# A hybrid decoder block on one core: the chunked delta rule multiplies its state by the keys themselves, and its last inverse level works in 64x64 blocks

## The chip, the core and the metric

The kernel runs on one core of a Trainium2 chip. The metric is the device time of one execution in microseconds. A difference of under 0.5%, about 8.6 us here, is about what a measurement of this kernel can't tell from no change.

## What is computed

One layer of a decoder block on 1024 positions of 1024 channels: an input projection, a gated delta rule (4 heads, 128 channels each), a sparse attention, a gated merge, a LayerNorm, a convolutional feed-forward part and a second LayerNorm. Only the delta rule is touched. Cut to it, the reference reads:

```python
gc = jnp.cumsum(g, axis=-1)                     # decay, summed within a chunk
diff = gc[..., :, None] - gc[..., None, :]
decay = jnp.where(tril, jnp.exp(jnp.where(tril, diff, 0.0)), 0.0)
kk = jnp.einsum('bhnid,bhnjd->bhnij', k, k)
a_mat = jnp.where(strict, kk * decay * beta[..., :, None], 0.0)
lhs = jnp.eye(c) + a_mat
rhs = jnp.concatenate([v * beta[..., None], k * (beta * jnp.exp(gc))[..., None]], -1)
sol = lax.linalg.triangular_solve(lhs, rhs, left_side=True, lower=True)
u0, kcd = sol[..., :dv], sol[..., dv:]
...
def step(state, xc):                            # over the chunks, in order
    u = u0_c - kcd_c @ state
    o = qd_c @ state + qk_c @ u
    state = state * gl_c + kd_c.T @ u
    return state, o
```

The kernel works in chunks of 128 positions, which gives the same result.

## The kernel before

TensorE's order is written by hand (`tc.manual_schedule(engines=MS)`, with TensorE alone in `MS`); the other engines' orders come from the scheduler of the framework, and each engine works strictly in its order.

The delta rule is cut into eight units: four heads `h` by two halves `hf` of four chunks. A unit has a preparation (`pre`, a generator) and a scan (`scan`, another), each of which stops at every `yield`. Between their pieces TensorE works on the input projection: a tile of it (a "fill", `proj_gen`) is 48 products of 512 columns in three passes of a split into a high and a low part (`xTh,wh`, `xTl,wh`, `xTh,wl`). `PLAN` says which fills belong to which of nine stretches (two to four fills each), and the tables `PRE` and `SCAN` say at which fraction of a stretch a piece of the preparation or the scan is put between the fills' products: unit n's preparation begins with stretch n, its scan in stretch n+1. A fill of q, k or v channels (`act_gen`) ends with a convolution on VectorE.

A preparation transposes k (L488), spreads the gates along rows with four products by the triangle `triu` (L504), builds the strictly lower triangular matrix `Am` (L523), inverts its 16x16 diagonal blocks on VectorE (L534 to L550, over two DMA round trips), and then builds the inverse `Z` of the whole 128x128 matrix in three levels of 16, 32 and 64 (L586 to L607). Each level is two groups of four products, one for each chunk:

```python
mm(ps[:, csl[c]], Am[:, c, :], Z[:, c, :])      # then times the level's mask, on VectorE: Y
mm(ps[:, csl[c]], X[:, c, :], Y[:, c, :])       # X = Z transposed; then Z = Z + this, on VectorE
```

Behind the last level the preparation multiplies the gated keys `kb` by the inverse (L610), and ScalarE copies the result, `kc`, out. The scan then takes for each chunk, with two stops, `u = Z v + kc S` as two products into one place (L625, L627), a copy of `u` on ScalarE (L629), the product `kd u` and the new state `S` from it on VectorE (L633, L638), and the two products of the output (L640, L642).

A name pair such as `sm<-Z,Am` in a row of TensorE is the output, the moving operand and the stationary operand (which the weight load brings in). One fp32 product is two records of a matmul in the trace.

## Time and profile before

| what | us |
|---|---|
| three runs | 1714.35, 1717.88, 1722.87 (median 1717.88) |
| the profiled execution, its time | 1719.78 |
| its span from the first to the last instruction | 1718.0 |
| TensorE busy in the span | 1675.0 (97%) |

The span leaves 1.8 us of the profiled execution's time around it. A busy TensorE is not TensorE at its peak: the ends of matmuls are modelled, and neighbours overlap, so what one more product costs is read from the starts of the instructions around it and not from its own duration.

### The profile page before, as it was taken

How to read it: one execution, taken by the hardware profiler on the slowest of the kernel's cores; microseconds unless marked ns; L12 is line 12 of the kernel's file. 1: busy time of each engine (PE TensorE's matmuls, PEld its weight loads, DVE VectorE, ACT ScalarE, POOL GpSimd, SP SyncE). 2: the span in 40 equal slices, each digit the busy share in tenths (PEclk: the TensorE clock that was granted, in tenths of full speed). 3: DMA queues.
4: the chain of work that ended last, by engine and by line, in shares of the span. 5: the costliest groups of instructions: out<-in, count | busy, mean ns of one | idle time of the engine just before them, and what ended most of it. 6: DMA issues, size and time to landing. Idle time of an engine off the chain costs nothing.

```text
span 1718.0 us, 23466 instructions
## 1 busy us (share of the span) xinstructions
PE 1675.0 (97%) x8562; PEld 1411.7 (82%) x8562; DVE 1116.2 (65%) x2089; ACT 734.2 (43%) x1269; POOL 788.1 (46%) x640
## 2 busy tenths in 40 slices
PE   8999999999999998999999999999999999999997
PEld 8888888888888877888877887788888888888885
DVE  3545647657433358899874328988677667865656
ACT  3422323223222458788843115544444444443333
POOL 1322222232212537887657236678877777210005
PEclk9999999999999999999999999999999999999998
DMA  5222121221221312334125612333332232687722
GB/s 177 75 63 76 56 66 45 61 75 33 87 81 52 98 63 96 126 105 132 35 87 184 224 58 89 111 107 116 118 104 93 98 112 98 215 315 269 234 88 98
DMA packets 199024, 189.88 MB, mean 111 GB/s; under 512 B 19656, under 2 KB 155005, under 8 KB 198909
## 3 DMA queue, kind: packets, MB, share of 16 engines
q1 hardware_dynamic: 198909, 188.39, 34.3%
q8 instruction: 67, 1.10, 0.3%
q14 instruction: 48, 0.39, 0.1%
HBM read 136.97 MB, written 51.38 MB: 110 GB/s over the span
## 4 chain that ended last, share of the span: by engine, by line
PE 82%; DVE 7%; issue 3%; ACT 3%; POOL 3%; DMA 2%; SPq 0%; ACTq 0%; POOLq 0%; DVEq 0%
PE pq L193 37%; PE big L193 29%; PE sm L193 12%; PE sm L983 2%; DVE st L917 1%; ACT P L919 1%; POOL P L872 1%; DVE wh L991 1%; DMA w<-in_w_out_dram 1%; DVE wl L991 1%; DVE st L881 0%; DVE wb L1454 0%; DMA w<-in_w_down_dram 0%; DMA wsum<-w 0%; PE big L247 0%
## 5 line engine op out<-in xcount | busy, mean ns | idle before, releaser
L183 POOL TENSOR_TENSOR wl<-w,wh 128x1024 fp32r<-128x1024 f32 (+2 forms) x51 | 123.1, 2418 | 362.1 <-PE big L193 132.9
L193 PE MATMUL big<-xTl,wh 128*128 128x512 f32 x608 | 244.1, 402 | 0.0
L193 PE MATMUL big<-xTh,wh 128*128 128x512 f32 x608 | 244.1, 401 | 0.0
L193 PE MATMUL pq<-wd 128*128 128x512 f32 x924 | 209.6, 389 | 0.0
L193 PEld LDWEIGHTS pq<-wd 128*128 128x128 f32 x924 | 173.4, 188 | 36.0
L193 PE MATMUL pq<-xb,wb 128*128 128x512 f32 x792 | 187.6, 391 | 2.0 <-DVE accs L1465 1.5
L1465 DVE SCALAR_TENSOR_TENSOR accs<-pq,fcw,accs 128x510 f32<-128x510 f32 (+3 forms) x264 | 144.5, 568 | 61.0 <-ACT accs L1553 56.1
L193 PEld LDWEIGHTS pq<-xb,wb 128*128 128x128 f32 x792 | 148.5, 188 | 34.8 <-issue 2.8
L193 PE MATMUL big<-xTh,wl 128*128 128x512 f32 x608 | 160.3, 399 | 0.0
L193 PEld LDWEIGHTS big<-xTl,wh 128*128 128x128 f32 x608 | 114.7, 189 | 20.7 <-issue 0.2
L193 PEld LDWEIGHTS big<-xTh,wh 128*128 128x128 f32 x608 | 114.7, 189 | 20.6
L193 PE MATMUL pq<-mTh,wb 128*128 128x512 f32 x528 | 127.6, 397 | 3.2 <-ACT mTh L1253 3.1
L193 PEld LDWEIGHTS big<-xTh,wl 128*128 128x128 f32 x608 | 110.9, 188 | 21.4
L193 PE MATMUL pq<-mTl,wb 128*128 128x512 f32 x528 | 127.3, 391 | 0.0
L872 POOL TENSOR_TENSOR P<-P,st 128x640 f32<-128x640 f32 (+6 forms) x94 | 106.3, 1160 | 45.1 <-DVE st L881 19.7
L193 PEld LDWEIGHTS pq<-mTh,wb 128*128 128x128 f32 x528 | 101.1, 192 | 25.8 <-ACT mTh L1253 3.3
L193 PEld LDWEIGHTS pq<-mTl,wb 128*128 128x128 f32 x528 | 99.1, 188 | 21.2
L1454 POOL TENSOR_TENSOR wb<-w,wb 128x512 fp32r<-128x512 f32 x79 | 103.7, 1319 | 27.2 <-ACT wb L1253 27.2
L182 ACT ACTIVATE wh<-w 128x1024 fp32r<-128x1024 f32 (+2 forms) x51 | 53.1, 1046 | 134.8 <-PE big L193 90.7
L193 PE MATMUL big<-kS,qS 128*128 128x320 f32 (+5 forms) x384 | 86.7, 343 | 3.2 <-ACT P L919 2.0
L919 ACT ACTIVATE P<-big,st 128x640 f32<-128x640 f32 (+6 forms) x112 | 83.3, 749 | 10.3 <-DVE st L917 9.5
L1253 ACT ACTIVATE wb<-w 128x512 fp32r<-128x512 f32 x85 | 53.3, 629 | 80.3 <-PE pq L193 76.0
(394 smaller groups left out, 3558.1 us busy)
## 6 DMA issues: line engine op xcount, KB each, us to landing
w<-in_w_in_dram SPq DMA_DIRECT2D x40, 512.0 KB, 3.9
w<-in_w_up_dram SPq DMA_DIRECT2D x36, 512.0 KB, 3.8
w<-in_w_down_dram SPq DMA_DIRECT2D x53, 256.0 KB, 3.7
wsum<-w SPq DMA_DIRECT2D x44, 256.0 KB, 2.5
sig<-th SPq DMA_DIRECT2D x32, 256.0 KB, 2.2
w<-sig SPq DMA_DIRECT2D x30, 256.0 KB, 3.3
wx<-in_w_up_dram SPq DMA_DIRECT2D x11, 512.0 KB, 3.8
gdrC<-accs SPq DMA_DIRECT2D x11, 512.0 KB, 2.6
```

The costliest lines, as they stand in the source:

```text
L182: A.activation(wh[:, :n], w[:, :n], AF.Copy)
L183: G.tensor_tensor(wl[:, :n], w[:, :n], wh[:, :n].bitcast(F32), op=OP.subtract)
L193: PE.matmul(o, a, b, start=start, stop=stop, skip_group_check=True)
L872: G.tensor_tensor(p, p, r.to_broadcast([128, p.shape[1]]), op=OP.mult)
L917: V.reduce_max(nm, pv if m > 1 else pv[:, 0], axis=AX.X, negate=True)
L919: A.activation(P[:, r0 + i, :n], pv[:, i], AF.Exp, bias=nm[:, i:i + 1], accum_out=su[:, i:i + 1])
L983: PE.transpose(tp[:n, r * 128:(r + 1) * 128], P[:, r, c0:c0 + n], ident)
L991: V.tensor_tensor(pl, tp[:n], ph.bitcast(F32), op=OP.subtract)
L1253: A.activation(o, i, AF.Copy)
L1454: e.tensor_tensor(H.tile[:, 1], src(), H.tile[:, 0].bitcast(F32), op=OP.subtract)
L1465: V.scalar_tensor_tensor(o, i, fcw[:, 2 - s, j:j + 1], o, op0=OP.mult, op1=OP.add)
```

## The change

Three edits in the delta rule, and the two tables of places.

1. **The state times the keys.** `kb` (POOL), its product with the inverse (four products), and the copy `kc` are gone. `kc` is now a copy of the transposed keys, made by ScalarE from SBUF. In the scan a chunk begins with the product of the state by `kc`, VectorE adds it, times the gate `nb`, to `vb` (a new `scalar_tensor_tensor`), and after one more stop the inverse is multiplied by that sum. So a chunk has three stops in place of two.
2. **Rows of gates.** At the start of the program the summed gates are split into a high and a low part, transposed once, and laid out as `grow` (64 rows by 512). A unit then makes its rows with one product of 512 columns by a selecting matrix `pick` of ones and zeros, in place of a copy on ScalarE (`gb`) and four products by `triu`.
3. **The last level in blocks of 64.** The masked whole products of level 64 become four transposes of 64x64, four products of 64 columns by `Am`, a copy of both, four products of 64x64 and a copy of the result into the upper right block of `Z`. The transposes of the whole `Z` after level 32, and two passes of VectorE with the mask, are gone.

`PRE` has 12 places in place of 14, `SCAN` 15 in place of 11, closer together. Some small tiles move to another pool (left out of the diff).

```diff
@@ -32,8 +32,8 @@
 Y0, Y1 = 10, 12
 WOS = [4, 5, 6, 7, 8, 9, 10, 11]
 UNITS = [(t, g) for t in (1, 2, 3, 4, 5, 6, 7, 0) for g in range(2)]
-PRE = [0.0, 0.04, 0.07, 0.1, 0.14, 0.2] + [0.72 + 0.05 * i for i in range(8)]
-SCAN = [1.13 + 0.085 * i for i in range(8)] + [1.81, 1.86, 1.92]
+PRE = [0.0, 0.04, 0.07, 0.1, 0.14, 0.2] + [0.74 + 0.06 * i for i in range(6)]
+SCAN = [1.11 + 0.058 * i for i in range(12)] + [1.82, 1.87, 1.93]
 
 
 def PLAN(z, M, QKV, F):
...
@@ -271,14 +271,14 @@
...
-    triu = gmask.tile([128, 128], F32, name="triu")
+    triu = xin.tile([128, 128], F32, name="triu")
...
-    for b in (16, 32, 64):
+    for b in (16, 32):
...
@@ -381,6 +381,22 @@
     V.tensor_tensor(egd, plv, gc, op=OP.subtract)
     A.activation(egd, egd, AF.Exp)
     A.activation(egc, gc, AF.Exp)
+    gcs = xin.tile([128, 2, NT, 4], F32R, name="gcs")
+    V.tensor_copy(gcs[:, 0], gc)
+    V.tensor_tensor(gcs[:, 1], gc, gcs[:, 0].bitcast(F32), op=OP.subtract)
+    both = xin.tile([64, 32], F32, name="both")
+    V.tensor_tensor(both, ident[:64, 0:32], ident[:64, 32:64], op=OP.add)
+    pick = gmask.tile([64, 2, 2, 4], F32R, name="pick")[:, 0]
+    pick32 = xin.tile([64, 2, 4], F32, name="pick32")
+    V.reduce_sum(pick32, both.rearrange("p (f c h) -> p f h c", f=2, c=4), axis=AX.X)
+    V.tensor_copy(pick, pick32)
+    chunk = xin.tile([64, 4], F32, name="chunk")
+    V.reduce_sum(chunk, both.rearrange("p (f c h) -> p c f h", f=2, c=4), axis=AX.XY)
+    ps = sm()
+    PE.transpose(ps[:64, :128], gcs.rearrange("p l t h -> p (l t h)").bitcast(F32), ident)
+    grow = gmask.tile([64, 4, 128], F32R, name="grow")
+    V.tensor_tensor(grow, ps[:64, None, :128].to_broadcast([64, 4, 128]),
+                    chunk[:, :, None].to_broadcast([64, 4, 128]), op=OP.mult)
 
     mhalf = const.tile([128, 1], F32, name="mhalf")
     V.memset(mhalf, -0.5)
@@ -497,11 +513,8 @@
             V.tensor_tensor(nb, bp, egc[:, cs, h], op=OP.mult)
             V.tensor_scalar(bv, bv, 0.5, None, op0=OP.mult)
             yield
-            gb = g5("tmp", 3)
-            A.activation(gb, gg[:, cs, h, None].to_broadcast([128, 4, 128]), AF.Copy)
             gr = sm()
-            for c in range(4):
-                mm(gr[:, csl[c]], gb[:, c, :], triu)
+            mm(gr, pick[:, hf, h:h + 1].to_broadcast([64, 128]), grow.rearrange("p c i -> p (c i)"))
             dS = g5("tmp", 3)
             for c in range(4):
                 V.scalar_tensor_tensor(dS[:, c], gr[:, csl[c]], gc[:, hf * 4 + c, h:h + 1], mds,
@@ -578,12 +591,12 @@
                 mm(kq[:, csl[c]], kT[:, tsl[c]], qT[:, tsl[c]])
             qk = g5("qk")
             V.tensor_tensor(qk, v4(kq), dT, op=OP.mult)
-            kb = g5("tmp", 3)
-            G.tensor_tensor(kb, kt, bc(nb), op=OP.mult)
+            kc = gp.tile([128, 512], F32, name="kc", tag="kc", bufs=2)
+            A.activation(kc, kT[:, hf * 512:(hf + 1) * 512], AF.Copy)
             kd = kt
             G.tensor_tensor(kd, kd, bc(egd[:, cs, h]), op=OP.mult)
             yield
-            for b in (16, 32, 64):
+            for b in (16, 32):
                 ps = sm()
                 for c in range(4):
                     mm(ps[:, csl[c]], Am[:, c, :], Z[:, c, :])
@@ -594,27 +607,27 @@
                 for c in range(4):
                     mm(ps[:, csl[c]], X[:, c, :], Y[:, c, :])
                 V.tensor_tensor(Z, v4(ps), Z, op=OP.add)
-                if b < 64:
+                if b == 16:
                     X = g5("X")
-                if b < 32:
                     V.transpose(X.rearrange("p c i -> p (c i)"), Z.rearrange("p c i -> p (c i)"))
                 yield
-                if b == 32:
-                    ps = sm()
-                    for c in range(4):
-                        PE.transpose(ps[:, csl[c]], Z[:, c, :], ident)
-                    A.activation(X, v4(ps), AF.Copy)
-                    yield
             ps = sm()
             for c in range(4):
-                mm(ps[:, csl[c]], kb[:, c, :], Z[:, c, :])
-            kc = g5("kc")
-            A.activation(kc, v4(ps), AF.Copy)
-            st[hf] = (Z, vb, kc, qk, qd, kd, rr, rq2)
+                PE.transpose(ps[:64, c * 64:c * 64 + 64], Z[:64, c, :64], ident[:64, :64])
+            for c in range(4):
+                mm(ps[:64, 256 + c * 64:320 + c * 64], Am[:, c, :64], Z[:, c, 64:])
+            XY = g5("X").rearrange("p c i -> p (c i)")
+            A.activation(XY[:64], ps[:64], AF.Copy)
             yield
+            ps = sm()
+            for c in range(4):
+                mm(ps[:64, c * 64:c * 64 + 64], XY[:64, c * 64:c * 64 + 64], XY[:64, 256 + c * 64:320 + c * 64])
+            A.activation(Z[:64, :, 64:], ps[:64, :256].rearrange("p (c i) -> p c i", c=4), AF.Copy)
+            st[hf] = (Z, vb, kc, nb, qk, qd, kd, rr, rq2)
+            yield
 
         def scan(h, hf, st):
-            Z, vb, kc, qk, qd, kd, rr, rq2 = st[hf]
+            Z, vb, kc, nb, qk, qd, kd, rr, rq2 = st[hf]
             S = st.get("S")
             o = sm()
             for c in range(4):
@@ -622,9 +635,12 @@
                     us = sm()
                 b0 = (c % 2) * 256
                 u_ps, s_ps = us[:, b0:b0 + 128], us[:, b0 + 128:b0 + 256]
-                mm(u_ps, Z[:, c, :], vb[:, c, :], True, S is None)
+                vn = vb[:, c, :]
                 if S is not None:
-                    mm(u_ps, kc[:, c, :], S, False, True)
+                    mm(s_ps, kc[:, csl[c]], S)
+                    V.scalar_tensor_tensor(vn, s_ps, nb[:, c:c + 1], vb[:, c, :], op0=OP.mult, op1=OP.add)
+                yield
+                mm(u_ps, Z[:, c, :], vn)
                 u = gp.tile([128, 128], F32, name="u", tag="u", bufs=2)
                 A.activation(u, u_ps, AF.Copy)
                 yield
```

What moves in TensorE's order is shown at unit 1. Before, its last level stands so between the fills' products (`big<-xTh` and `big<-xTl`; L605 transposes `Z`, L488 the keys of the next unit):

```order
L605 MATMUL sm<-ident,Z 128x128 x4
L193 MATMUL big<-xTh_83,wl 128x512 x7
L193 MATMUL big<-xTh_85,wl 128x512 x3
L193 MATMUL sm<-Z,Am 128x128 x4
L193 MATMUL big<-xTh_85,wl 128x512 x5
L488 MATMUL sm<-ident,sil 128x128 x4
L193 MATMUL big<-xTh_83,wh 128x512
L193 MATMUL big<-xTl_84,wh 128x512
L193 MATMUL big<-xTh_83,wh 128x512
L193 MATMUL sm<-Y,X 128x128 x4
```

In the changed kernel the same place reads (L616 are the transposes of 64x64, `sm<-X` the four products of 64x64, `grow,pick` the rows of gates of the next unit):

```order
L616 MATMUL sm<-ident,Z 64x64 x4
L193 MATMUL sm<-Z,Am 64x64 x4
L193 MATMUL big<-xTh_85,wl 128x512 x3
L504 MATMUL sm<-ident,sil 128x128 x4
L193 MATMUL big<-xTh_83,wh 128x512
L193 MATMUL big<-xTl_84,wh 128x512
L193 MATMUL big<-xTh_83,wh 128x512
L193 MATMUL big<-xTl_84,wh 128x512
L193 MATMUL big<-xTh_83,wh 128x512
L193 MATMUL big<-xTl_84,wh 128x512
L193 MATMUL sm<-X 64x64 x4
L193 MATMUL sm<-grow,pick 128x512
```

The two groups of the level are now short ones, the whole products by `X` have gone, and the one product by `pick` stands where four by `triu` stood. The tile of the array that the built program names is 64x64 for `ident,Z` and `sm<-X`, 128x64 (rows by columns) for the `Z,Am` between fills here, 64x128 for `grow,pick`, and 128x128 for the other rows of these two pieces.

The second place is the scan of the same unit on TensorE. Before, one chunk from the product with the state (`S,kc`) to the products that read `u`:

```order
L193 MATMUL sm<-vb,Z 128x128
L193 MATMUL sm<-S,kc 128x128
L193 MATMUL big<-xTh_85,wl 128x512 x4
L193 MATMUL big<-xTh_83,wh 128x512
L193 MATMUL big<-xTl_84,wh 128x512
L193 MATMUL big<-xTh_83,wh 128x512
L193 MATMUL big<-xTl_84,wh 128x512
L193 MATMUL big<-xTh_83,wh 128x512
L193 MATMUL big<-xTl_84,wh 128x512
L193 MATMUL big<-xTh_83,wh 128x512
L193 MATMUL big<-xTl_84,wh 128x512
L193 MATMUL sm<-u,kt 128x128
```

After, from the same product to the product with the inverse, and the fills behind it:

```order
L193 MATMUL sm<-S,kc 128x128
L193 MATMUL big<-xTh_85,wl 128x512 x7
L193 MATMUL big<-xTh_83,wh 128x512
L193 MATMUL big<-xTl_84,wh 128x512
L193 MATMUL sm<-vb,Z 128x128
L193 MATMUL big<-xTh_83,wh 128x512
L193 MATMUL big<-xTl_84,wh 128x512
L193 MATMUL big<-xTh_83,wh 128x512
L193 MATMUL big<-xTl_84,wh 128x512
```

`vb,Z` no longer stands beside `S,kc` but nine products of the fills later, since it now reads what VectorE makes of `S,kc`.

The third place is VectorE while unit 4's scan meets the convolution of a fill (`sil`). The new rows are L641; L654 is the state update that was L638, L568 the transpose of `Z` that waits for a DMA:

```order
L654 SCALAR_TENSOR_TENSOR S<-S,egl,sm 128x128
L475 SCALAR_TENSOR_TENSOR sil<-big,gcw,sil 128x509
L641 SCALAR_TENSOR_TENSOR vb<-sm,sc,vb 128x128
L479 SCALAR_TENSOR_TENSOR sil<-th,sil 128x512
L545 COPY XB<-eye 32x256
L475 SCALAR_TENSOR_TENSOR sil<-big,gcw,sil 128x512 x2
L568 STREAM_TRANSPOSE X<-Z 128x512
L475 SCALAR_TENSOR_TENSOR sil<-big,gcw,sil 128x512
L654 SCALAR_TENSOR_TENSOR S<-S,egl,sm 128x128
L479 SCALAR_TENSOR_TENSOR sil<-th,sil 128x512
L641 SCALAR_TENSOR_TENSOR vb<-sm,sc,vb 128x128
```

Each chunk now has two rows of the scan on this engine, with the convolution's rows between them.

## Rows read from the trace of the kernel before

**Rows 1.** The page: span, the line of the engines' busy times, and the first line of the chain that ended last (shares of the span by engine).

```profile
span 1718.0 us, 23466 instructions
...
PE 1675.0 (97%) x8562; PEld 1411.7 (82%) x8562; DVE 1116.2 (65%) x2089; ACT 734.2 (43%) x1269; POOL 788.1 (46%) x640
...
PE 82%; DVE 7%; issue 3%; ACT 3%; POOL 3%; DMA 2%; SPq 0%; ACTq 0%; POOLq 0%; DVEq 0%
```

**Rows 2.** Busy time of each engine in the stretch from 55 to 540 us, which holds the whole delta rule (start, end, length, then busy us and records of PE, PEld, DVE, ACT, POOL, then granted clock, DMA share and GB/s).

```profile
55.00:540.00 485.00, 483.89 (x2662) 414.46 (x2662) 265.47 (x716) 136.43 (x228) 120.19 (x72) 1.00 0.22 63
```

**Rows 3.** Who kept TensorE's matmuls (first line) and its weight loads (other lines) waiting between 50 and 560 us: us in total, times, longest.

```profile
PE sm L193 <- DVE Z L596: 1.0, 2, 0.5
...
PEld sm L193 <- DVE Z L596: 1.9, 2, 0.9
PEld sm L193 <- ACT tmp L501: 0.5, 1, 0.5
```

**Rows 4.** TensorE in order of time, at a group of four full fp32 products between products of the projection (start us, duration us, then the instruction; x8 counts records, two for each fp32 product).

```profile
135.41 0.39 PE L193 MATMUL big<-xTl,wh 128*128 128x512 f32 x1
135.63 1.05 PE L193 MATMUL sm<-Y,X 128*128 128x128 f32 x8
136.44 0.48 PE L193 MATMUL big<-xTh,wh 128*128 128x512 f32 x1
136.76 0.39 PE L193 MATMUL big<-xTl,wh 128*128 128x512 f32 x1
```

**Rows 5.** The same at a group of four 128x128 transposes.

```profile
150.90 0.40 PE L193 MATMUL big<-xTl,wh 128*128 128x512 f32 x1
...
151.82 0.39 PE L193 MATMUL big<-xTl,wh 128*128 128x512 f32 x1
152.05 0.60 PE L559 MATMUL sm<-ident,sil 128*128 128x128 f32 x4
152.40 0.48 PE L193 MATMUL big<-xTh,wh 128*128 128x512 f32 x1
152.72 0.40 PE L193 MATMUL big<-xTl,wh 128*128 128x512 f32 x1
```

**Rows 6.** The same at two fp32 products whose stationary operand has 64 columns and whose moving operand has 64 (x4: two records for each), in the attention's compression after the delta rule; the last line is their weight loads.

```profile
616.24 0.40 PE L193 MATMUL sm<-xTh,wh 128*128 128x512 f32 x1
616.57 0.45 PE L193 MATMUL sm<-w2s,hTc 128*64 128x64 f32 x4
616.94 0.50 PE L193 MATMUL sm<-xTl,wh 128*128 128x512 f32 x1
617.28 0.40 PE L193 MATMUL sm<-xTh,wh 128*128 128x512 f32 x1
...
616.57 0.31 PEld L193 LDWEIGHTS sm<-w2s,hTc 128*64 128x64 f32 x4 [0.36 <-issue]
```

**Rows 7.** The same at one transpose of 32 rows, before the delta rule.

```profile
50.47 0.40 PE L193 MATMUL big<-xTl,wh 128*128 128x512 f32 x1
50.79 0.24 PE L329 MATMUL sm<-ident,st 32*128 32x32 f32 x1
50.97 0.51 PE L193 MATMUL big<-xTh,wh 128*128 128x512 f32 x1
51.31 0.40 PE L193 MATMUL big<-xTl,wh 128*128 128x512 f32 x1
```

**Rows 8.** Three state updates of the scan, each as the product that it waits for on TensorE and its start on VectorE; for the first and the last also the next product that reads the new state (start us, duration us, the instruction).

```profile
387.45 0.38 PE L193 MATMUL sm<-u,kt 128*128 128x128 f32 x2
389.33 0.34 DVE L638 SCALAR_TENSOR_TENSOR S<-S,egl,sm 128x128 f32<-128x128 f32 x1
391.32 0.39 PE L193 MATMUL sm<-S,kc 128*128 128x128 f32 x2
...
429.63 0.39 PE L193 MATMUL sm<-u,kt 128*128 128x128 f32 x2
430.06 0.35 DVE L638 SCALAR_TENSOR_TENSOR S<-S,egl,sm 128x128 f32<-128x128 f32 x1 [0.84 <-PE sm L193]
...
436.30 0.38 PE L193 MATMUL sm<-u,kt 128*128 128x128 f32 x2
438.85 0.31 DVE L638 SCALAR_TENSOR_TENSOR S<-S,egl,sm 128x128 f32<-128x128 f32 x1
440.17 0.39 PE L193 MATMUL sm<-S,kc 128*128 128x128 f32 x2
```

**Rows 9.** Groups of instructions by line and shape (xcount | busy us, mean ns of one | idle before, releaser).

```profile
L591 DVE TENSOR_TENSOR Y<-sm,lev 128x512 f32<-128x512 f32 x24 | 16.6, 691 | 69.2 <-PE sm L193 69.2
L638 DVE SCALAR_TENSOR_TENSOR S<-S,egl,sm 128x128 f32<-128x128 f32 x24 | 8.1, 338 | 21.7 <-PE sm L193 21.7
...
L612 ACT ACTIVATE kc<-sm 128x512 f32<-128x512 f32 x8 | 4.8, 595 | 3.3 <-PE sm L193 3.3
```

**Rows 10.** The start of the delta rule's work: the first product of the second fill on TensorE and the first convolution passes of the first fill on VectorE (start us, duration us).

```profile
57.05 0.39 PE L193 MATMUL big<-xTh,wh 128*128 128x512 f32 x1
...
57.98 2.32 DVE L459 SCALAR_TENSOR_TENSOR sil<-big,gcw,sil 128x511 f32<-128x511 f32 x3 [2.01 <-ACT sil L456]
```

More of the change, by code (lines that the diff above doesn't have):

```diff
@@ L222, in hybrid_block_kernel @@
     vS = S6.tile([128, NT, 2, 4, 64], F32R, name="vS", tag="s")
-    sp = gmask.tile([128, NT, 32], F32, name="sp")
+    sp = xin.tile([128, NT, 32], F32, name="sp")
     def load_x(tt):
@@ L346, in hybrid_block_kernel @@
     dtb = row_bcast(gdn_dt_bias, 4, "dtb")
-    av = ctile("av", [NT, 4])
+    av = xin.tile([128, NT, 4], F32, name="av")
     V.tensor_tensor(av, sp[:, :, 28:32], dtb[:, None, :].to_broadcast([128, NT, 4]), op=OP.add)
-    s0 = ctile("s0", [NT, 4])
-    s1 = ctile("s1", [NT, 4])
-    s2 = ctile("s2", [NT, 4])
-    s3 = ctile("s3", [NT, 4])
+    s0 = xin.tile([128, NT, 4], F32, name="s0")
+    s1 = xin.tile([128, NT, 4], F32, name="s1")
+    s2 = xin.tile([128, NT, 4], F32, name="s2")
+    s3 = xin.tile([128, NT, 4], F32, name="s3")
     A.activation(s0, av, AF.Abs)
```

## Prediction

> **What bounds the kernel now.** I read the page first: TensorE is busy for 97% of the span, and 82% of the chain that ended last is its own [rows 1]. A share over the whole span says nothing of one stage, so I took the stretch of the delta rule alone. From 55 to 540 us TensorE is busy for 483.9 of 485.0 us, at a granted clock of 1.00, while VectorE works 265, ScalarE 136 and POOL 120 us [rows 2]. The waits agree: in that stretch TensorE waited about 1 us for VectorE, its weight loads 1.9 us, and 0.5 us once for ScalarE's copy of the gates (L501) [rows 3]. So the projection's fills hide the whole chain of preparation and scan. A product taken from TensorE here is worth its slot, and work taken from another engine is worth nothing by itself. What follows the delta rule has the same order of instructions on TensorE in both kernels, and should only move earlier.
>
> **What a slot costs.** I read the starts of neighbours, not durations. Products of the fills start every 0.23 us (150.90 to 151.82, four steps) [rows 5]. A group of four whole fp32 products lengthens the way between two fill products from two steps (0.46) to 1.35 us (135.41 to 136.76): 0.89 us [rows 4]. Four whole transposes take 0.90 - 0.46 = 0.44 us in the same way [rows 5].
>
> **What is removed, per unit.** Both groups of level 64, the product with `kb`, and the four products by `triu`: 4 x 0.89 = 3.56 us, and the transposes of `Z`, 0.44: together 4.00, for eight units 32.0 us.
>
> **What is added.** Per unit one product by `pick`, 512 columns like a fill's, 0.23 us, and short ones: four transposes (one record each) and eight fp32 products (two records each), 20 records of 64 columns. The nearest row is the group of 64-column products: its four weight loads take 0.31 us together [rows 6], so a record takes at most 0.08; half of a whole product's record (0.89 / 8 / 2) is 0.055. I take 0.06, since the group's loads include a first one that overlaps nothing. So 0.23 + 20 x 0.06 = 1.43 per unit, 11.4 us in all. The scan keeps its number of products; they only stand apart.
>
> **The price of a new shape.** That group of 64-column products costs 617.28 - 616.24 - 0.46 = 0.58 us, of which four records are 0.24. The other 0.34 lies at its two edges: the fill ahead is followed after 0.33 us and not 0.23, and the weight load waits 0.36 us as issue [rows 6]. One transpose of 32 rows shows the same from the row side: 0.84 - 0.46 = 0.38, less 0.06, is 0.32 [rows 7]. So each change of the array's tile costs about 0.17 us. In the order of the changed kernel I count 49 of them: three at every pair `ident,Z` and `Z,Am`, three at every pair of `sm<-X` and `grow,pick`, and two each for the first `pick` and the last `sm<-X`, which stand alone. That makes 8.3 us. It is the term that I trust least: the rows show groups of one shape between fills, none with a second shape inside.
> The Trainium skill (TensorEngine Tiling (Array Packing), Tiling Modes) says that changing the tiling mode, and not just the tile, drains TensorE. By it the inner changes count too, as I have counted them; were only the edges of the 17 groups paid, the term would be 17 x 0.34 = 5.8 us, and no run here tells the two apart yet.
>
> **The new round trip.** In 28 chunks the product with the state must now go through VectorE before the inverse can use it. The new pass has the shape of the state's update, 0.34 us [rows 9]; sixteen passes of 0.69 us like `Y` go away with the level, so VectorE's load stays [rows 9]. What counts is the wait of TensorE, with all fills queued behind it. With nothing ahead of it, the update starts 0.43 us after its product [rows 8], so a trip needs 0.43 + 0.34 = 0.77 us. In the piece of unit 1 shown, nine fill products stand between `S,kc` and `vb,Z`: 9 x 0.23 + 0.22 for the product itself (a quarter of 0.89) = 2.29 us. That leaves 1.5 us for other rows of VectorE. Where a convolution is queued, an update started 1.88 us after its product, and at 436.30 one started 2.55 us after: held up by 1.45 and 2.12 us [rows 8]. The second would have stalled TensorE by 0.6 us in the new spacing; it is the worst that I found against its room. Twice as many such trips, with the convolution's rows between them (the third place in the order), might meet this two to four times: I take 2 us. Bounds: none, and 28 x 0.6 = 17 us.
>
> **Costed at nothing, and what covers it.** ScalarE gives up three passes of 0.6 us per unit (L612 is one [rows 9]) and gets two and a short one; POOL loses `kb`. Both have slack [rows 2]. At the start VectorE's first convolution stands behind `grow`, which waits for a transpose 13 products into the second fill: 57.05 + 3.0, so about 3 us after its old start at 57.98 [rows 10]. Two banks and a fill of 48 x 0.23 = 11 us cover that; without that cover the price is 1 us by estimate. The wait for L501 (0.5 us) goes [rows 3].
>
> **The sum.** 32.0 - 11.4 - 8.3 = 12.3 us off TensorE; less 2 for stalls, plus 0.5, less 0.3 for the start: 10.5 us. From the profiled execution, 1719.8 us (span 1718.0 [rows 1] and 1.8 around it), that is 1709.3. The median of the three runs is 1717.9, 1.9 lower, and gives 1707.4. I say 1708.
>
> **Rivals.**
> *The short products bring nothing.* If a record of 64 columns keeps the slot of a whole one (0.11), 20 of them cost 2.2 us and the added part 19.4 in place of 11.4. Then 10.5 - 8 = 2.5 us remain: 1715, no change that can be told. For it: edges are dear. Against it: the four loads in 0.31 us [rows 6]. The same end is reached if stalls take 6 us more.
> *A change of tile is free in this place*, because neighbours overlap in the queue: 10.5 + 8.3 = 18.8 us, 1699. Against it: both groups that show a change pay for it [rows 6, 7].
> *Slower: VectorE becomes the scan's bound.* Its mechanism is the new pass queued behind convolution passes, three units of which meet a scan, and behind the transpose that waits for a DMA. The gain of 12.3 us is used up at 12.3 / 28 = 0.44 us of stall per trip, and the kernel is slower by over 0.5% (8.6 us) from 0.75 us each: about 1727. For it: two hold-ups of 1.45 and 2.12 us [rows 8]. Against it: TensorE waits for hardly anything now [rows 3], and most trips fall where VectorE is half idle [rows 2].
>
> **Chances and range.** A gain of 8.6 to 15 us, the forecast: 0.50. More, with cheap changes of shape: 0.09. Under 8.6 us either way, with dear short products or stalls: 0.35. Slower by more: 0.06. So faster 0.59, the same 0.35, slower 0.06, with 0.5% (8.6 us) as the bound that a measurement can tell. The range of 1700 to 1715 leaves out the slower case, the part of the third case without a gain, and the far end of the cheap one: some 0.2 together.
>
> **What will show it.** Right: from 55 us to the scan's end some 10 us less, later stages unchanged in length; `sm<-X` groups that cost about 0.6 to 0.8 us between fills; TensorE's waits for VectorE's L641 of 1 to 4 us in total. Wrong: waits for L641 above 8 us, which would be the slower rival; short groups at 0.9 us or more, the first rival; short groups at 0.5 us with no longer step at their edges, the second.

## The result, and the profile after

The changed kernel takes 1708.05 us (median of 7 runs, 1702.83 to 1712.13) against 1718.99 us for the kernel before on the same chip (7 runs, 1714.35 to 1726.0). The ratio is 0.9919, with a 95% interval of 0.9902 to 0.9935: 0.65 to 0.98% faster. (The two medians alone lie 10.9 us apart, 0.64%, just below the small end of that interval.) The profiled execution took 1708.62 us, its span is 1706.9 us.

The page after, in the lines that answer to [rows 1]:

```profile
span 1706.9 us, 23176 instructions
...
PE 1661.8 (97%) x8443; PEld 1391.5 (82%) x8443; DVE 1118.6 (66%) x2106; ACT 734.0 (43%) x1269; POOL 778.1 (46%) x630
```

TensorE lost 13.2 us of busy time, VectorE gained 2.4. (The line of the chain is left out: in this trace the chain can be followed back only to 531 us, near the end of the delta rule, so its shares add up to 67% of the span and can't be set beside those of before.)

In the stretch of [rows 2] TensorE is still all but full, at a granted clock of 1.00:

```profile
55.00:540.00 485.00, 482.89 (x2597) 403.72 (x2596) 271.61 (x743) 138.84 (x232) 114.94 (x66) 1.00 0.23 65
```

So the stage must have become shorter, and two marks show by how much. What I call the stage below reaches from the first fill product to the first product `sm<-wh,Ck`, which stands behind the scan. On TensorE's timeline of the kernel after:

```profile
44.87 0.50 PE L193 MATMUL big<-xTh,wh 128*128 128x512 f32 x1
...
545.06 0.28 PE L193 MATMUL sm<-wh,Ck 128*128 128x256 f32 x1
```

and of the kernel before:

```profile
45.08 0.51 PE L193 MATMUL big<-xTh,wh 128*128 128x512 f32 x1
...
557.17 0.28 PE L193 MATMUL sm<-wh,Ck 128*128 128x256 f32 x1
```

500.2 us after, 512.1 before: 11.9 us. The span is 11.1 us shorter. Behind the mark every engine has the same instructions in the same order in both kernels, and the attention took 255.4 us after and 255.6 before.

Who kept TensorE waiting between 50 and 560 us (first two lines: its products; the others: its weight loads; us in total, times, longest), against [rows 3]:

```profile
PE sm L583 <- DVE sil L479: 1.7, 1, 1.7
PE sm L677 <- DVE tmp L672: 0.3, 1, 0.3
...
PEld sm L616 <- issue: 2.9, 8, 0.4
...
PEld sm L193 <- DVE S L654: 1.3, 3, 0.5
```

VectorE's new pass (L641) is not in the list. What came in are other waits: the transposes of v (L583) once wait for the end of v's convolution (L479), three products wait for the state's update (L654), and eight times the weight loads of the 64x64 transposes (L616) begin late by `issue`, as the load at the new tile shape of [rows 6] did.

### The profile page after: what moved, and what is told of

Read it like the earlier page. It is cut to its first block, busy times and chain, and to the rows that moved or that the text cites. A ratio compares the mean times of both kernels' runs of the same rounds, so it can differ in the third digit from the quotient of the medians.

```text
span 1706.9 us, 23176 instructions
## 1 busy us (share of the span) xinstructions
PE 1661.8 (97%) x8443; PEld 1391.5 (82%) x8443; DVE 1118.6 (66%) x2106; ACT 734.0 (43%) x1269; POOL 778.1 (46%) x630
## 4 chain that ended last, share of the span: by engine, by line
PE 48%; DVE 8%; issue 3%; POOL 3%; ACT 3%; DMA 2%; SPq 0%; POOLq 0%; DVEq 0%; ACTq 0%
PE pq L193 35%; PE big L193 7%; PE sm L193 5%; PE sm L999 2%; DVE st L933 1%; ACT P L935 1%; DVE wh L1007 1%; DVE wl L1007 0%; DVE wb L1470 0%; DMA wsum<-w 0%; DMA w<-in_w_out_dram 0%; DVE st L897 0%; POOL h L1327 0%; POOL h L1328 0%; DVE accs L1481 0%
## 5 line engine op out<-in xcount | busy, mean ns | idle before, releaser
L193 PE MATMUL big<-xTh,wl 128*128 128x512 f32 x608 | 164.7, 402 | 0.0
L935 ACT ACTIVATE P<-big,st 128x640 f32<-128x640 f32 (+6 forms) x112 | 83.2, 748 | 10.8 <-DVE st L933 10.2
```

The costliest lines, as they stand in the source:

```text
L193: PE.matmul(o, a, b, start=start, stop=stop, skip_group_check=True)
L935: A.activation(P[:, r0 + i, :n], pv[:, i], AF.Exp, bias=nm[:, i:i + 1], accum_out=su[:, i:i + 1])
```

## The experiments

The stage is the finer measure: it differs by 0.3 us between two profiles of one and the same kernel (first edit alone, below; the only repeat), where the timed medians of two groups of ten runs of that kernel, on two chips, lie 4.3 us apart. It has one blemish. In four of the profiles (group taken apart; full tiles; no third edit; fewer shapes, v later) TensorE waited once for 1.92 to 2.44 us inside the stage, and its granted clock was then 0.50 (1.2 GHz) for 3.4 us. That is worth up to 1.7 us of these four stages; the others, before and changed among them, ran at 1.00 throughout. All results in one table; ratios are against the kernel before on the same chip.

| kernel | stage, us | against before | time, us | ratio, 95% interval |
|---|---|---|---|---|
| before | 512.1 | | | |
| changed | 500.2 | -11.9 | 1708.05 | 0.9919 (0.9902 to 0.9935) |
| first edit alone | 505.9 | -6.2 | 1720.99 | 1.0001 (0.9988 to 1.0015) |
| the same once more | 506.2 | -5.9 | 1716.66 | 0.9965 (0.9951 to 0.9980) |
| second edit alone | 509.3 | -2.8 | 1721.13 | 0.9998 (0.9981 to 1.0016) |
| third edit alone | 514.4 | +2.3 | 1723.84 | 1.0025 (1.0010 to 1.0039) |
| group taken apart | 522.2 | +10.1 | 1727.17 | 1.0035 (1.0015 to 1.0054) |
| fewer shapes | 498.9 | -13.2 | 1707.72 | 0.9929 (0.9906 to 0.9953) |
| full tiles | 508.4 | -3.7 | 1713.73 | 0.9962 (0.9946 to 0.9978) |
| two passes | 504.3 | -7.8 | 1714.65 | 0.9966 (0.9951 to 0.9981) |
| shifted | 505.5 | -6.6 | 1712.77 | 0.9961 (0.9947 to 0.9975) |
| no third edit | 503.2 | -8.9 | 1706.73 | 0.9917 (0.9899 to 0.9935) |
| fewer shapes, v later | 502.0 | -10.1 | 1709.10 | 0.9927 (0.9912 to 0.9942) |
| tight scan | 503.0 | -9.1 | 1710.83 | 0.9939 (0.9916 to 0.9961) |

**Each edit alone, in the kernel before.** First the state times the keys, with its places:

```
-            kb = g5("tmp", 3)
-            G.tensor_tensor(kb, kt, bc(nb), op=OP.mult)
+            kc = gp.tile([128, 512], F32, name="kc", tag="kc", bufs=2)
+            A.activation(kc, kT[:, hf * 512:(hf + 1) * 512], AF.Copy)
...
+                    mm(s_ps, kc[:, csl[c]], S)
+                    V.scalar_tensor_tensor(vn, s_ps, nb[:, c:c + 1], vb[:, c, :], op0=OP.mult, op1=OP.add)
+                yield
+                mm(u_ps, Z[:, c, :], vn)
```

> The kernel before with the first edit alone: the state times the keys, VectorE's pass, and the scan spread over fifteen places; the gates' products by `triu` and the level of 64 stay as they were. Theory (slots removed, less stalls): four whole products per unit go, 8 x 0.89 = 7.1 us, no tile shape changes, one to three us of stalls come in: the first product `sm<-wh,Ck` behind the scan, which starts at 557.2 us in the kernel before, starts at 551 to 553, and the time is 4 to 6 us shorter. Rival (VectorE becomes the scan's bound): the 28 trips cost 0.44 us each or more, so the stage is as long as before or longer, and TensorE waits 12 us or more for the pass of VectorE on the state's product.

The stage is 6.2 us shorter, and TensorE all but never waits for VectorE's pass (one weight load, 0.2 us): the slots are there, nearly in full. The time did not follow; I come back to that below.

The second, the rows of gates:

```
-            gb = g5("tmp", 3)
-            A.activation(gb, gg[:, cs, h, None].to_broadcast([128, 4, 128]), AF.Copy)
...
-                mm(gr[:, csl[c]], gb[:, c, :], triu)
+            mm(gr, pick[:, hf, h:h + 1].to_broadcast([64, 128]), grow.rearrange("p c i -> p (c i)"))
```

> The kernel before with the second edit alone: the rows of gates by one product with `pick`, everything else as before. Theory: 8 x (0.89 - 0.23) = 5.3 us of slots go, 16 changes of tile shape at 0.17 us cost 2.7, and 0.5 us of wait for the copy of the gates goes: the first `sm<-wh,Ck` at 554 us, 3 us earlier than 557.2. Rival (a change of shape is free): 5.8 us earlier, 551.4. In the time neither can be told from no change; the trace decides.

The stage is 2.8 us shorter, as the theory had it. The time did not follow here either; the attention of this profile took 259.9 us, 4.3 more than before.

The third, with twelve places and one for `kb`:

```
-            for b in (16, 32, 64):
+            for b in (16, 32):
...
+                PE.transpose(ps[:64, c * 64:c * 64 + 64], Z[:64, c, :64], ident[:64, :64])
+                mm(ps[:64, 256 + c * 64:320 + c * 64], Am[:, c, :64], Z[:, c, 64:])
```

> The kernel before with the third edit alone: the level of 64 in blocks, everything else as before. Theory: eight whole products and four whole transposes per unit go, 8 x (1.78 + 0.44) = 17.8 us; 20 short records per unit come, 9.6 us by 0.06 each; 40 changes of tile shape at 0.17 us, 6.8 us: 1.4 us earlier, the first `sm<-wh,Ck` at 555.8. Rival (changes are free): 8.2 us earlier, 549. Rival (a short record costs what a whole one does, 0.11): 6.6 us later, 563.8.

2.3 us longer, which none of the three had. TensorE's weight loads show why, in one line:

```profile
PEld sm L193 <- ACT tmp L501: 6.8, 8, 1.2
```

[Rows 3] had 0.5 us here, once; now it is all eight units (the products themselves waited 3.1 us in five of them). ScalarE copies the gates (L501) behind the square of the keys (L491), and that starts when VectorE has copied the transposed keys (L489). VectorE's copy and ScalarE around one of them:

```profile
204.12 0.69 DVE L489 COPY kt<-sm 128x512 f32<-128x512 f32 x1 [5.06 <-PE sm L488]
203.89 0.37 ACT L612 ACTIVATE Z<-sm 64x256 f32<-64x256 f32 x1
204.84 0.60 ACT L491 ACTIVATE tmp<-sm 128x512 f32<-128x512 f32 x1 [0.58 <-DVE kt L489]
205.34 0.62 ACT L501 ACTIVATE tmp<-gg 128x512 f32<-128x512 f32 x1
```

and TensorE, whose product by `triu` starts at 206.01 and not at 205.3:

```profile
205.08 0.40 PE L193 MATMUL big<-xTl,wh 128*128 128x512 f32 x1
206.01 1.16 PE L193 MATMUL sm<-triu,tmp 128*128 128x128 f32 x8 [0.54 <-ACT tmp L501]
```

The level's own copy (L612) is not what holds them up: it ends at 204.26, and ScalarE is then idle for 0.58 us. What has changed is TensorE's order. Before, four whole products of the level (`sm<-Y,X`) stood between the keys' transposes and the products by `triu`; now fill products stand there alone, six at this place, which is less time than the copies need. The places that I chose put the group and the keys' transposes next to each other, so the wait belongs to this order as much as to the edit. It goes some way to explain why the three single gains (6.2 + 2.8 - 2.3 = 6.7 us) add up to less than the whole (11.9): the second edit does away with the very copy that is late here. The seven changes of shape fewer that the whole has, against the single edits together, are another part (1.2 us at 0.17 each).

**The price of a new shape.** The same work, the group taken apart, each piece at a place of its own (`PRE` has as many more places):

```
                 PE.transpose(ps[:64, c * 64:c * 64 + 64], Z[:64, c, :64], ident[:64, :64])
+                yield
             for c in range(4):
                 mm(ps[:64, 256 + c * 64:320 + c * 64], Am[:, c, :64], Z[:, c, 64:])
+                if c < 3:
+                    yield
```

> The changed kernel with the group `ident,Z` and `Z,Am` of each unit taken apart: each of its four transposes and four products stands alone among products of the fills, the work is the same. 104 more changes of tile shape (153 in place of 49). Theory (each change costs 0.17 us, by the two edges of a lone group): 17.7 us longer than the changed kernel, the first `sm<-wh,Ck` at 563 in place of 545.1, the time about 1726. Rival (changes free where neighbours overlap in the queue): within 2 us of the changed kernel, 545 to 547 and 1708 to 1710.

The stage is 22.0 us longer than the changed kernel's. From the starts of the neighbours the pieces cost 17.4 us more, 0.17 for each of the 104 changes. The rest is waits (TensorE's products waited 3.1 us more for VectorE, 3.7 of it at the new pass, less elsewhere) and the clock behind the longest of them. One lone product shows the price directly:

```profile
144.07 0.40 PE L193 MATMUL big<-xTl,wh 128*128 128x512 f32 x1
144.40 0.33 PE L193 MATMUL sm<-Z,Am 128*64 128x64 f32 x2
144.66 0.50 PE L193 MATMUL big<-xTh,wh 128*128 128x512 f32 x1
145.00 0.40 PE L193 MATMUL big<-xTl,wh 128*128 128x512 f32 x1
```

0.93 - 0.46 = 0.47 us for two records that cost 0.12: 0.35 for two changes. "Changes are free" is refuted.

The other way round, 17 changes fewer:

```
-    pick = gmask.tile([64, 2, 2, 4], F32R, name="pick")[:, 0]
+    pick = gmask.tile([128, 2, 2, 4], F32R, name="pick")[:, 0]
...
-                mm(ps[:64, 256 + c * 64:320 + c * 64], Am[:, c, :64], Z[:, c, 64:])
+                mm(ps[:64, 256 + c * 64:320 + c * 64], Am[64:, c, :64], Z[64:, c, 64:])
```

> The changed kernel with the work of its products unchanged but 17 fewer changes of tile shape (32 in place of 49): `pick` and `grow` are filled up with zeros to 128 rows, so that their product has the shape of a fill, and `Z,Am` takes only the rows 64 to 127 that hold anything, which gives it the shape of the transposes ahead of it. Theory (0.17 us for each change, those inside a group too): the first `sm<-wh,Ck` starts at 542.2 us in place of 545.1. Rival (only the edges of a group cost, and the inner change is free): 8 of the 17 count, those of the lone `pick` products, at most 1.4 us: 543.7 or later.

The stage is 1.3 us shorter. By itself that is the rival's figure (1.4 at most), and not the theory's 2.9. The groups say more. The first `pick` of the changed kernel, alone between fills:

```profile
91.99 0.40 PE L193 MATMUL big<-xTl,wh 128*128 128x512 f32 x1
92.31 0.49 PE L193 MATMUL sm<-grow,pick 64*128 64x512 f32 x1
92.73 0.50 PE L193 MATMUL big<-xTh,wh 128*128 128x512 f32 x1
93.08 0.39 PE L193 MATMUL big<-xTl,wh 128*128 128x512 f32 x1
```

and padded to 128 rows:

```profile
91.53 0.40 PE L193 MATMUL big<-xTl,wh 128*128 128x512 f32 x1
91.76 0.40 PE L193 MATMUL sm<-grow,pick 128*128 128x512 f32 x1
92.00 0.39 PE L193 MATMUL big<-xTh,wh 128*128 128x512 f32 x1
92.22 0.39 PE L193 MATMUL big<-xTl,wh 128*128 128x512 f32 x1
```

0.63 us against 0.23: two changes, 0.20 each. The pair of `sm<-X` and `pick` costs 1.23 us with three changes and 1.04 with two, so a change within a pair costs too, 0.19. The pair of `ident,Z` and `Z,Am` gave nothing back. In the changed kernel, then in this one:

```profile
140.74 0.41 PE L616 MATMUL sm<-ident,Z 64*64 64x64 f32 x4
141.08 0.68 PE L193 MATMUL sm<-Z,Am 128*64 128x64 f32 x8
141.69 0.97 PE L193 MATMUL big<-xTh,wl 128*128 128x512 f32 x3
```

```profile
139.89 0.41 PE L618 MATMUL sm<-ident,Z 64*64 64x64 f32 x4
140.23 0.67 PE L193 MATMUL sm<-Z,Am 64*64 64x64 f32 x8
140.84 0.97 PE L193 MATMUL big<-xTh,wl 128*128 128x512 f32 x3
```

The steps are the same, 0.34 and 0.61 us, and by the fills around it the pair costs 1.16 us in both. `Z,Am` now has the shape of the transposes, but sits on other rows of the array, 64 to 127 and not 0 to 63, and going from one to the other costs as much as the change to 128x64 did. So only nine of the 17 changes were saved: 7 x 0.19 + 0.40 = 1.7 us. The state's update took back 0.6 (the wait of its weight loads rose from 1.3 to 1.9), which leaves 1.1 of the 1.3 measured. Theory and rival both counted wrongly.

Last, no new shape at all, with moving operands of 64 columns on the whole array:

```
-                PE.transpose(ps[:64, c * 64:c * 64 + 64], Z[:64, c, :64], ident[:64, :64])
+                mm(ps[:, c * 64:c * 64 + 64], Z[:, c, :], ident[:, :64])
...
-                mm(ps[:64, 256 + c * 64:320 + c * 64], Am[:, c, :64], Z[:, c, 64:])
+                mm(ps[:, 256 + c * 64:320 + c * 64], Am[:, c, :], Z[:, c, 64:])
```

> The changed kernel without any new shape of tile: `pick` padded to 128 rows, and the level of 64 by products that use the whole array but move only 64 columns (whole `Z` against 64 columns of the identity, whole `Am`, and `X` with what stands beside it; rows that nobody reads come out too). 49 changes go, 8.3 us; eight identity records of 64 columns take the place of four short transposes, 4 x 8 x 0.06 = 1.9 us more. Theory: the first `sm<-wh,Ck` at 545.1 - 6.4 = 538.7 us, the time near 1702. Rival (on the whole array a record of 64 columns costs what one of 128 does, 0.11 us): 24 x 8 x 0.05 = 9.6 us more, 548.3, and the time near 1711.

The stage is 8.2 us longer than the changed kernel's, so the rival wins. TensorE's products and then their weight loads:

```profile
143.69 0.40 PE L193 MATMUL big<-xTl,wh 128*128 128x512 f32 x1
143.92 1.00 PE L193 MATMUL sm<-X 128*128 128x64 f32 x8
144.73 0.48 PE L193 MATMUL sm<-grow,pick 128*128 128x512 f32 x1
145.05 0.39 PE L193 MATMUL big<-xTh,wh 128*128 128x512 f32 x1
...
143.69 1.09 PEld L193 LDWEIGHTS sm<-X 128*128 128x128 f32 x8
```

From 143.69 to 145.05 are 1.36 us; less two fill steps (the padded `pick` takes one) that is 0.90 for eight records, what a whole group costs [rows 4], though half as many columns move. In the changed kernel the same group on 64x64 tiles loads its weights faster:

```profile
144.88 0.54 PEld L193 LDWEIGHTS sm<-X 64*64 64x64 f32 x8 [0.36 <-ACT tmp L507]
```

0.07 us a load against 0.14. A short record is cheap only where its stationary operand is small too. By this the theory's -6.4 becomes +3.2. Of the remaining 5 us TensorE's products waited 1.8 longer than in the changed kernel (2.8 us of their waits are for the state's update, 1.92 of that at once), and the clock at 0.50 behind that wait is worth up to 1.7; some 1.5 I can't place.

**The round trip.** Two passes in place of one:

```
-                    V.scalar_tensor_tensor(vn, s_ps, nb[:, c:c + 1], vb[:, c, :], op0=OP.mult, op1=OP.add)
+                    V.tensor_scalar(s_ps, s_ps, nb[:, c:c + 1], None, op0=OP.mult)
+                    V.tensor_tensor(vn, s_ps, vb[:, c, :], op=OP.add)
```

> The changed kernel with VectorE's pass on the state's product done in two passes, one that multiplies in place and one that adds: 28 x 0.34 = 9.5 us more work for VectorE, and each round trip longer by that. Theory (nine fill products cover the trip): TensorE's waits for this line stay under 2 us in total, and the first `sm<-wh,Ck` starts at 545 to 547 us. Rival (VectorE bounds the scan): each trip adds its 0.34 us, 554.6.

The stage is 4.1 us longer, with 4.0 us of waits of the weight loads for that line (the products themselves 2.3), in four of the 28 trips. Neither: VectorE doesn't bound the scan, yet the cover has holes. Where, the changed kernel's trips show. An ordinary one (product with the state, VectorE's pass, the product that needs it):

```profile
469.40 0.39 PE L193 MATMUL sm<-S,kc 128*128 128x128 f32 x2
469.82 0.35 DVE L641 SCALAR_TENSOR_TENSOR vb<-sm,sc,vb 128x128 f32<-128x128 f32 x1 [0.89 <-PE sm L193]
471.69 0.38 PE L193 MATMUL sm<-vb,Z 128*128 128x128 f32 x2
```

0.42 + 0.35 us, with 1.52 to spare. And the tightest, behind a transpose that waited for its DMA and behind a pass of the convolution:

```profile
168.89 0.38 PE L193 MATMUL sm<-S,kc 128*128 128x128 f32 x2
170.08 0.71 DVE L568 STREAM_TRANSPOSE X<-Z 128x512 f32<-128x512 f32 x1 [0.91 <-DMA Z<-zimg]
170.72 0.65 DVE L479 SCALAR_TENSOR_TENSOR sil<-th,sil 128x512 f32<-128x512 f32 x1
171.29 0.34 DVE L641 SCALAR_TENSOR_TENSOR vb<-sm,sc,vb 128x128 f32<-128x128 f32 x1
171.86 0.38 PE L193 MATMUL sm<-vb,Z 128*128 128x128 f32 x2
```

0.23 us to spare. So the cover was taken away on purpose:

```
-SCAN = [1.11 + 0.058 * i for i in range(12)] + [1.82, 1.87, 1.93]
+SCAN = [1.11 + 0.03 * i for i in range(12)] + [1.82, 1.87, 1.93]
```

> The changed kernel with the scan's twelve places 0.030 of a stretch apart in place of 0.058: four to five fill products fewer between the product with the state and the product that uses VectorE's result, so each trip has 0.9 to 1.2 us less room. In the changed kernel the 28 passes of VectorE end 0.2 to 4.3 us before TensorE needs them, half of them under 1.5 us. Theory (the fills' products are the cover of the trip): with 1.1 us less, five or six trips come late, 2.7 us of waits for that line in total, and the stage is 503 us in place of 500.2. Rival (the trips would be covered anyway, by whatever stands there): no waits for that line, 500 us. Rival (held-up trips push each other on): 8 us of waits or more, 508 us.

503.0 us, the theory's figure. Its parts are not: the weight loads wait for that line 4.4 us in ten trips (the products themselves 1.1), where 2.7 us in five or six were forecast, so the agreement to 0.1 us is partly luck. That the fills between are what pays for the trip is borne out; both rivals are out.

**Is a gain handed on?** The first edit's 6.2 us did not reach the time at first, and attention, with the same instructions, was 9.3 us longer than before. Two tries:

```
+            ps = sm()
+            for i in range(23):
+                mm(ps, xT["h", 0][:, i % 8, :128], xT["h", 1][:, i % 8, :])
     gmask_cm.close()
```

> The changed kernel with 23 products of 512 columns that nobody reads (23 x 0.229 = 5.3 us) put behind the scan, so that what follows starts where it starts in the kernel with the first edit alone: the first `sm<-wh,Ck` at 550.3 us. In that kernel the stage of attention (from the first `big<-kS,qS` to the first `big<-oAh,wh`) took 264.9 us at a granted clock of 0.95, against 255.4 at 0.98 in the changed one, with the same instructions in the same order on every engine. Theory (a delay is handed on as it is, and the longer stage belongs to that execution): the stage takes 255 to 257 us, and the time is 1713.3. Rival (the stage's length depends on when it starts): 260 us or more, and the time 1718 or more.

The stage grew by 5.3 us, attention took 255.6, the median time rose by 4.7: a delay is handed on as it is.

> The kernel with the first edit alone once more. Its stage was 6.2 us shorter than before's (505.9 against 512.1 us from the first fill product to the first `sm<-wh,Ck`), and nothing of that reached the time: attention took 264.9 us at a granted clock of 0.95. Theory (the loss belonged to that execution's clock): the stage is 505 to 507 us again, attention is back at 255 to 258 us, and the time is about 1715. Rival (the loss belongs to the kernel): attention is 260 us or more again at a clock under 0.97, and the time is 1719 or more.

Attention's row in the first profile of that kernel, then in the second (busy times in the order of [rows 2]; the last but two is the granted clock):

```profile
614.90:879.80 264.90, 247.90 (x1564) 215.73 (x1563) 228.42 (x400) 201.46 (x455) 184.12 (x189) 0.95 0.25 81
```

```profile
615.20:871.00 255.80, 237.18 (x1563) 207.22 (x1562) 226.64 (x396) 200.70 (x453) 184.00 (x189) 0.99 0.26 83
```

The second time attention was as long as in nine of the other twelve profiles (255.1 to 256.9 us) and the time fell by 4.9 us against before. So the loss of the first profile belonged to that execution, not to the kernel; the second edit alone (259.9 us) and the run without the third edit (261.4) had one too, and fewer shapes with v later a gain (251.9). The next pieces are from the end of attention in the first profile:

```profile
862.90:866.90 4.00, 1.89 (x9) 0.95 (x7) 3.90 (x8) 3.24 (x13) 4.00 (x4) 1.00 0.00 0
...
870.90:874.90 4.00, 4.00 (x18) 3.34 (x16) 1.32 (x4) 2.88 (x11) 1.70 (x4) 0.50 0.01 2
874.90:878.90 4.00, 4.00 (x21) 4.00 (x20) 3.00 (x6) 0.29 (x1) 0.49 (x2) 0.50 0.01 4
```

TensorE idled for 2.1 of 4 us, and then worked at 0.50, the level of 1.2 GHz, for at least 8 us. In the second profile it idled for 2.1 us between 858 and 866 us, behind the same line of VectorE, and kept 1.00. In all, the first attention had 24.8 us at 0.50 and the second 3.4, which is worth up to 10.7 us. But the clock is not the whole account: the changed kernel's attention had 10.2 us at 0.50 and took 255.4. Why the clock fell in one and not in the other stays open, and so does whether the first ten runs all lost their time there: their mean clock is lower (0.991 against 0.994), but only one of them has a trace, the slowest of the ten. What is shown is that medians of ten runs of one kernel can lie 4.3 us apart, on two chips, while those of the kernel before beside them were nearly equal (1720.17 and 1721.54); the two intervals do not meet. A ratio of 0.996 or 1.000 from ten runs says less than its interval claims.

**What is the third edit worth?** The first two edits with `pick` padded, and the level of 64 by whole products:

```
-            for b in (16, 32):
+            for b in (16, 32, 64):
```

> The first two edits without the third, with `pick` padded to 128 rows: no new shape of tile, the level of 64 by whole products as before. Theory: 6.2 us by the first edit, 2.8 by the second, 8 x 0.40 = 3.2 for the changes of shape that the padding takes away: a stage of 512.1 - 12.2 = 499.9 us, as long as the changed kernel's (500.2), the time 1707 to 1710. So the third edit would be worth only what padding is worth. Rival (the third edit is where the gain lies, 17.8 us of whole products removed, and it pays once VectorE and ScalarE are relieved by the other two): 505 us or more, the time 1713 or more.

The stage is 3.0 us longer than the changed kernel's, 3.3 above the forecast: the weight loads' waits of 3.2 us for the state's update and 1.1 for ScalarE's exponent of the gates (L531) stand in it, and the clock at 0.50 behind the longest, worth up to 1.7. Neither forecast fits. The time is the same as the changed kernel's within what the intervals tell, and from the starts of the neighbours the level and the gates cost 19.8 us here against 19.3. So of the three edits the third is the one that can be left out at little loss: it removes the most products and gives back nearly all of it in short records and changes of shape.

**A better order?** Fewer shapes, with the wait of the v transposes taken away:

```
-PRE = [0.0, 0.04, 0.07, 0.1, 0.14, 0.2] + [0.74 + 0.06 * i for i in range(6)]
+PRE = [0.0, 0.04, 0.07, 0.1, 0.2, 0.24] + [0.74 + 0.06 * i for i in range(6)]
```

> The changed kernel with 17 fewer changes of tile shape (as in the run with padded `pick` and `Z,Am` on rows 64 to 127) and the transposes of v moved from 0.14 to 0.20 of a unit's stretch, the product of keys and queries from 0.20 to 0.24. The wait of the v transposes for the convolution of v in the sixth unit, 2.2 us, should go: a stage of 498.9 - 1.9 = 497 us against 500.2 in the changed kernel, and the time 1704 to 1706. If another row of VectorE takes the place of that wait: 498.9.

502.0 us, above both forecasts. The wait at L583 is gone, and another took its place:

```profile
PEld sm L193 <- DVE vb L643: 4.6, 4, 2.9
```

Four trips of the scan now come late, and TensorE's products wait 3.0 us for them. The latest of them, on VectorE, with a pass of POOL beside it; the last line is the stretch behind it:

```profile
276.26 2.36 POOL L183 TENSOR_TENSOR wl<-w,wh 128x1024 fp32r<-128x1024 f32 x1 [10.51 <-PE big L193]
276.67 2.50 DVE L481 SCALAR_TENSOR_TENSOR sil<-th,sil 128x512 f32<-128x512 f32 x1
279.09 0.34 DVE L643 SCALAR_TENSOR_TENSOR vb<-sm,sc,vb 128x128 f32<-128x128 f32 x1
...
280.70:284.10 3.40, 3.40 (x10) 2.66 (x9) 0.92 (x2) 1.21 (x2) 0.00 (x0) 0.50 0.39 117
```

Its product with the state started at 273.89, its use at 279.48, 2.44 us after TensorE was ready for it. VectorE first stood behind a transpose that waited for a DMA. Then the convolution's pass (L481) took 2.50 us, though it has the shape of the one that took 0.65 above: it had begun while POOL's `wl<-w,wh` ran, and ended 0.55 us after it. In all fourteen traces 13 of the 336 passes `sil<-th,sil` took over 1.6 us; each began while a `wl<-w,wh` ran and ended 0.54 to 0.55 us after it. No run here moves either pass, so that POOL holds VectorE up is what the traces point to, not a tested cause. Behind the wait the clock was 0.50 for 3.4 us, worth up to 1.7. The 498.9 us of the kernel with fewer shapes, less 1.7 at L583, plus 3.0 and 1.7, are 501.9: that accounts for the stage, and most of it is this one meeting. By the time the kernel is no better than the changed one, and nothing that I ran is measurably so.

## Why the prediction was right, point by point

**What bounds the kernel.** Right: TensorE is full in the stage before and after, and what is taken from it is gained.

**The slots.** The sum had 32.0 us off and 19.7 on (11.4 + 8.3). The groups of the changed kernel give 8 x 1.16 for `ident,Z` with `Z,Am`, 7 x 1.23 for `sm<-X` with `pick`, and 0.63 and 0.81 for the two that stand alone: 19.3. Net 12.7 where 12.3 was forecast.

**The short records.** 0.06 us was right. The reason, half the moving columns, was only half of it: at 64 moving columns with a whole stationary operand a record costs 0.11. The row that I had used [rows 6] had both small.

**The price of a new shape.** The term that I trusted least held: 0.20 at a lone `pick`, 0.17 by the group taken apart, 0.19 inside the pair of `sm<-X` and `pick`. Paying the edges alone would have made 5.8 us of the 8.3. The Trainium skill (TensorEngine Tiling (Array Packing), Tiling Modes) says that changing the mode, and not just the tile, drains TensorE. The traces agree that a change of mode costs time, inside a pair too (1.23 us against 1.04). They differ at `Z,Am` on rows 64 to 127: there only the tile changed, and the pair cost the 1.16 us that it cost with a change of mode.

**The round trip.** The trip itself was right (0.42 + 0.35 us for 0.77 forecast), and the hold-ups came as feared: the latest pass started 2.40 us after its product, held up by 1.98 (1.45 and 2.12 were the rows before). The step that failed is the place of the 2 us of stalls: I put them at L641, where there are none. The late ones still fitted, one with 0.23 us to spare. The stalls came at the neighbours on the same engine: the v transposes behind the convolution and the state's updates behind it, 1.7 and 1.3 us. The prediction had not asked what is queued behind the new pass there. For the state's updates that is the new pass's doing as far as is known (with the first edit alone they waited 1.9 us). For the v transposes it is not: neither the first edit alone nor the run without the third edit has that wait, and its cause stays open. That the stalls came to about the 2 us of the sum, elsewhere, is luck.

**Costed at nothing.** ScalarE's copies of the level were covered. At the start VectorE's first convolution began 3.6 us later than before (61.61 us against 57.98) and TensorE did not wait, so the 0.3 us of the sum was not needed. The prediction priced the removal of the gates' copy at 0.5 us, by [rows 3]; beside the third edit alone TensorE's products waited 3.1 us for that copy.

**The sum.** 10.5 us forecast, 11.9 in the stage, 11.1 in the span. The rows give 12.7 of slots, and stalls of at most 2.9 (1.7 at L583, 0.3 at L677, and three products with the state that take up to 0.53 us in place of 0.23) against 1.0 before [rows 3], so 10.8. The other 1.1 us I can't assign.

**The rivals.** "Short products bring nothing" needed 0.11 a record, and has 0.06. "Changes are free" is refuted. "VectorE becomes the bound" needed 0.44 us at each of 28 trips; there was no wait, and even a pass twice as long made 4.0 us of waits in four trips.

## What to carry to other kernels

Read a new instruction's cost from starts of neighbours, in both kernels, and mind both operands: on TensorE a short product pays only if its stationary operand shrinks too, and each change of tile takes back about 0.17 to 0.20 us. A round trip over another engine is free as long as the independent work between its two ends is longer than the longest queue on that engine, so list the trips' slack and not their mean; and look at what stands behind the new pass, since the stall may come there. Judge an edit of a few microseconds by the length of its stage, but read the granted clock in it first: a wait of some 2 us was followed by 3.4 us at half the clock in four of these profiles. And try edits together as well as alone, because one can remove the wait that another makes.

## What the runs showed of the hardware that I had not expected

- An fp32 record of 64 moving columns takes 0.11 us with a stationary operand of 128x128, as one of 128 moving columns does, and 0.06 us on a 64x64 tile; the weight loads took 1.09 us for eight and 0.54.
- Going from a 64x64 tile on rows 0 to 63 to one on rows 64 to 127 took as long as going to a 128x64 tile (steps of 0.34 and 0.61 us in both). A lone product of 64 rows, padded with zeros to 128, cost 0.40 us less.
- Single waits of TensorE of 1.92, 1.95, 2.35 and 2.44 us inside the stage were each followed by 3.4 us at a granted clock of 0.50, in four executions; one of 2.0 us (L583 in the run with two passes) was not.
- A pass of VectorE that takes 0.65 to 0.69 us took 1.67 to 2.76 when it began while POOL's `wl<-w,wh` ran, and ended 0.54 to 0.55 us after that, 13 times in fourteen traces.
- After an idle stretch at the end of attention TensorE was granted 0.50 for at least 8 us in one execution and 1.00 in another of the same kernel. Two times ten runs of that kernel gave ratios of 1.0001 and 0.9965.
